# Which rows are gathered when, and on which engine the value products run, in a one-step hybrid decoder

## The chip, the cores and the metric

One core of a Trainium2 chip runs the whole program. Its engines are TensorE (PE; PEld is its weight load), VectorE (DVE), ScalarE (ACT), GpSimd (POOL), which here only issues gathers, and SyncE (SP), which issues all other transfers. The metric is the time of one execution on the device in microseconds, the median of several runs. Everything is single precision. Most matrix products are made of three in a rounded format, each operand being split into a high part (H) and a low rest (L): H by H, H by L, L by H.

## What is computed

A decoder layer over 1024 prompt tokens and 64 sampled tokens: a state-space branch, attention in three dilated windows, a gated mix, an output projection, and then the part that the change touches, a channel mixer that retrieves experts. For each token, eight heads choose 16 of 16384 experts each, so 128 rows of two tables:

```python
eidx = jnp.take_along_axis(cidx, pos, axis=-1).reshape(TOKEN_BLOCK, PEER_HEADS * PEER_TOPK)
gate = jax.nn.softmax(best, axis=-1).reshape(TOKEN_BLOCK, PEER_HEADS * PEER_TOPK)
ue = jnp.take(u_tab, eidx, axis=0)
act = jax.nn.gelu(jnp.einsum('td,tkd->tk', xb, ue))
ve = jnp.take(v_tab, eidx, axis=0)
return jnp.einsum('tk,tkd->td', (gate * act).astype(xb.dtype), ve)
```

The result is added to the layer's input and normalised.

## The kernel before

The tokens go in two halves. The first half is 512 prompt tokens (with the 64 sampled ones up to the attention); the second half is the other 512 and the 64. The second half's experts are computed densely, over all 16384 of them, on TensorE (`dense`); the first half's are gathered, token by token. The gathers are a side stream: the generator `gather` yields after each gathered row, and `tick` advances it by the rate in force (`pace`, the table `RATES`) while the second half's main work is written out. So the order of instructions on each engine is set when the program is built, by these rates and by a scheduler that places the instructions; on the chip each engine then runs its list in order.

The gathered half is four tiles of 128 tokens. For a tile, `gather_u` fetches 128 pieces; a piece is one row of `u_tab` for each of 128 tokens, 512 KB in a buffer `row` (8 buffers, shared by everything gathered), issued by POOL (line 1559). VectorE forms a dot product of each token's row with its input (line 1563, a "dot"). After 128 dots the weights are ready (`act`, line 1569, and for product tiles on TensorE their transpose `wT`).

Then the value rows. There are two ways. In `gather_v` a piece holds one token's 128 rows on 128 partitions (line 1625); for four tokens at a time VectorE copies their weights into `strips` (line 1636) and TensorE forms the products into `va` (line 1641, a "group" of 16 profile entries). In `gather_w`, used for the tiles in `VT`, a piece holds one row for each of 128 tokens (line 1591), and VectorE multiplies it by the token's weight and adds it to the sum `x3v` (line 1597, an "add"). `x3v` is a buffer of the dense loop, so adds can't start before it; there is one such buffer, loaded with the tile's input (line 1587) and sent out after normalising (line 1605). The row of u and the row of v that come next are chosen by a difference of counts, `LEAD`.

The main work beside it, in order: attention of the second half, gated mixing (`glu`), output projection (`w_out`, line 1223), norms, queries (16 chunks: a product, then the top 16 of 128 scores on VectorE, lines 1304 to 1308), the choice of experts (`choose`), the gates (comparisons `oij` on VectorE at line 1392, scaled on ScalarE, multiplied on TensorE, copied into `Gt` and written out; some of the dense scores are computed early between them), and the dense loop (scores, weights `a` times G at line 1442, split at 187, products, accumulation at lines 1464 and 1462), then the last norms (lines 1497 to 1504).

Of the kernel before, what the change touches and what calls it, by code (L numbers as in the profile page):

```python
# [8 lines left out]
I32 = mybir.dt.int32  # L9
# [25 lines left out]
ATICK = 2.8  # L35
LAG, SMB = 4, 5
FILL = (1.1, 2.274, 0.0, 0.8, 1.5, 0.05)
RATES = (1.0, 1.3, 1.0, 1.0, 0.86, 1.0, 0.6)
RB = 8
GL = 20  # L40
GO = (2, 0, 0.7)
LEAD = 160

VT = (2, 3)
SSMT = (10.0, 0.0, 5.0)
NS = 2

# [20 lines left out]
class Prog:  # L68
    def __init__(self, tc, a, stop=None):
        self.tc, self.nc, self.a, self.stop = tc, tc.nc, a, stop  # L70
        self.marks = []
        self.sides, self.inside, self.last, self.dn = {}, False, None, None

    def mark(self, name):
        n = [i.name for i in self.nc.cur_bb.bb.instructions[-1:]]
# [7 lines left out]

        self.sides[name] = [gen, rate, 0.0]

    def pace(self, name, rate):
        if name in self.sides:
            self.sides[name][1] = rate

    def tick(self, us):  # L90
        if self.inside:
# [439 lines left out]
    def mix(self, h):  # L531
        tc, nc = self.tc, self.nc
        nt = NT[h]
        if h == 0:
            self.attn_ahead(0)
        with tc.tile_pool(name=f"at{h}", bufs=1) as ap:
            attn = (ap.tile([128, 4, nt], F32R, name="atH"), ap.tile([128, 4, nt], F32R, name="atL"))
            self.mark(f"attn{h}")
            if h == 0:
                with tc.tile_pool(name="sa", bufs=1) as sp:  # L540
                    self.beside("samples", self.sample_attention(sp), FILL[0])
                    self.attention(h, attn)
                    self.drain("samples")
            else:
                self.pace("gather", RATES[0])
                oa = ap.tile([128, 4, 64], F32, name="oa")
                nc.sync.dma_start(oa, self.oa)
                self.split(attn[0][:, :, 512:], attn[1][:, :, 512:], oa)
                self.attention(h, attn)
                self.pace("gather", RATES[1])  # L550
            with tc.tile_pool(name=f"mx{h}", bufs=1) as mp:
                mix = (mp.tile([128, 8, nt], F32R, name="mixH"), mp.tile([128, 8, nt], F32R, name="mixL"))
                self.mark(f"glu{h}")
                self.glu(h, attn, mix)
                if h == 0:
                    self.es1 = ExitStack()
                    self.ahd1 = [self.es1.enter_context(tc.tile_pool(name=n, bufs=1, side="right")) for n in ("xp1", "pj1")]
                    self.beside("ahead", self.ahead(), FILL[5])
                if h:
                    self.pace("gather", RATES[5])  # L560
                self.mark(f"wout{h}")
                self.espx, px = self.right(f"px{h}")
                self.xf = (px.tile([128, 8, nt], F32R, name="x2H"), px.tile([128, 8, nt], F32R, name="x2L"))
                self.esx2, xp = self.right(f"x2p{h}")
                g = xp.tile([128, D], F32, name="gffn")
                nc.sync.dma_start(g, self.a["g_ffn"].to_broadcast([128, D]))
                x2 = self.w_out(h, mix, xp)
        self.x2sb = xp, g, x2
# [663 lines left out]
    def peer_keys(self, h):  # L1232
        tc, nc, a = self.tc, self.nc, self.a
        v = nc.vector
        nt = NT[h]
        ntl = len(TILES[NT[h]])
        es2 = ExitStack()
        self.pace(*(("gather", RATES[6]) if h else ("ahead", FILL[1])))
        x, (xp, g, x2) = self.xf, self.x2sb
        with ExitStack() as es:  # L1240
            esj = ExitStack()
            jk = esj.enter_context(tc.tile_pool(name=f"jk{h}", bufs=1, side="left" if h else "right"))
            for i in range(ntl):
                rows = 128 if i < 4 else 64
                r0 = h * 512 + i * 128 if i < 4 else 1024
                xn = jk.tile([128, D], F32, name="xn", tag="xn", bufs=2 + h)[128 - rows:]
                self.rms(xp, x2[i][128 - rows:], g[128 - rows:], xn, xn)
                if h == 0:
                    nc.sync.dma_start(self.xn2[r0:r0 + rows], xn)
                self.to_t(xn, rows, x, i * 128, 128 - rows)  # L1250
                self.tick(4.0)
            esj.close()
            self.esx2.close()
            if h:
                da = es.enter_context(tc.tile_pool(name="da", bufs=1))
            with tc.tile_pool(name=f"pk{h}", bufs=1, side="right") as kp, ExitStack() as eg:
                self.pace(*(("gather", RATES[2]) if h else ("ahead", FILL[2])))
                sv = [kp.tile([128, 16, 16], F32, name=f"sv{i}") for i in range(ntl)]
                si = [kp.tile([128, 16, 16], U32, name=f"si{i}") for i in range(ntl)]
                kq = eg.enter_context(tc.tile_pool(name=f"kq{h}", bufs=1, side="right"))  # L1260
                for c in range(16):
                    qp = kq.tile([128, nt], F32, name="qp", tag="qp", bufs=2)
                    keys = kq.tile([128, 128], F32, name="keys", tag="keys", bufs=3)
                    nc.sync.dma_start(keys, a["keys"][:, c])
                    for ps, (c0, c1) in zip(self.gemm_f(a["w_qp"][c], x, SPLITS[NT[h]]), SPLITS[NT[h]]):
                        nc.scalar.copy(qp[:, c0:c1], ps[:, :c1 - c0])
                    pvs = []
                    for i in range(ntl):
                        rows = 128 if i < 4 else 64
                        if i % 4 == 0:  # L1270
                            ps = self.trt()
                        pvs.append(ps[:rows, (i % 4) * 128:(i % 4) * 128 + 128])
                        self.mm(pvs[i], qp[:, i * 128:i * 128 + rows], keys, start=True, stop=True)
                    for i in range(ntl):
                        rows = 128 if i < 4 else 64
                        rest = kq.tile([128, 128], F32, name="rest", tag="rest", bufs=3)[:rows]
                        self.top16(sv[i][:rows, c], si[i][:rows, c], pvs[i], rest)
                    self.tick(6.0)
                    if h and c in CE:
                        self.early(da, x)  # L1280
                self.pace(*(("gather", RATES[3]) if h else ("ahead", FILL[3])))
                eg.close()
                if h:
                    kg = eg.enter_context(tc.tile_pool(name="kg", bufs=1, side="right"))
                for i in range(ntl):
                    rows = 128 if i < 4 else 64
                    self.choose(kp, h, i, rows, sv[i], si[i], (lambda: self.early(da, x)) if h else None)
                    if h == 0:
                        self.tick(30.0)
                    if h == 0 and i == GO[0]:  # L1290
                        self.beside("gather", self.gather(), GO[1])
                    if h:
                        self.gates(kg, i, rows, lambda: self.early(da, x))
            if h:
                self.mark("dense")
                self.pace("gather", RATES[4])
                dn = self.dn = es2.enter_context(tc.tile_pool(name="dn", bufs=1, side="right"))
                self.dense(dn, da, x)
                es2.close()
        self.espx.close()  # L1300
# [206 lines left out]
    def gather(self):  # L1507
# [10 lines left out]
        nu = nv = 0  # L1518
        made = [0, 0]
        while nv < 4:  # L1520
            can = [nu < 4 and nu < nv + 3, nv < nu and (nv not in VT or self.dn is not None)]
            if not any(can):
                yield RATE
                continue
            pick = int(made[0] - made[1] >= LEAD)
            if not can[pick]:
                pick = 1 - pick
            made[pick] += 1
            if next((us[nu] if pick == 0 else ws[nv]), None) is None:
                nu, nv = nu + 1 - pick, nv + pick  # L1530
            else:
                self.catch_up(2)
                yield RATE
# [13 lines left out]
    def gather_u(self, i):  # L1547
# [3 lines left out]
        xn = gp.tile([128, D], F32, name="gxn", tag="gxn", bufs=1)  # L1551
        nc.sync.dma_start(xn, self.xn2[i * 128:(i + 1) * 128])

        ei = self.ei[i] = gp.tile([128, 128], I32, name="ei", tag="ei", bufs=2)
        v.tensor_copy(ei, ef)
        act = gp.tile([128, 128], F32, name="act", tag="act", bufs=3)
        for k in range(128):
# [50 lines left out]
    def gather_v(self, i):  # L1608
# [2 lines left out]

        ps = self.trt()
        nc.tensor.transpose(ps[:, :128], self.peer[0, i][1], self.ident)
        eT = gp.tile([128, 128], I32, name="eT", tag="eT", bufs=2)
        v.tensor_copy(eT, ps[:, :128])
        for hf in range(2):

# [128 lines left out]
```

## Time and profile before

| | us |
|---|---|
| median of 3 runs (3988.77 to 4004.48) | 3997.65 |
| profiled execution | 4006.35 |
| its span | 4004.6 |
| PE busy | 3737.3 |
| DVE busy | 2937.0 |
| POOL busy | 1421.8 |
| dots, x512 (L1563) | 618.0 |
| adds, x256 (L1597) | 327.8 |

Busy time is the time in which an engine has an instruction under way; a mean over the span hides that different stages have different limits. A line of a helper stands for many operations, so the line 80 is most of TensorE's work. The granted clock is 1.00 where TensorE ran at 2.4 GHz throughout.

### The profile page before, as it was taken

Reading aid. Unit: us, or ns where it says so; the run is one execution under the profiler, and the core shown is the slowest. Engines: PE = TensorE matmul, PEld = TensorE weight load, DVE = VectorE, ACT = ScalarE, POOL = GpSimd, SP = SyncE. Lnnn points to the kernel's source line nnn. Section 1 sums busy time; section 2 is a strip of 40 time slices with the busy share of each in tenths; the row PEclk is TensorE's granted clock in tenths of the full one; section 3 lists DMA queues with packets and bytes.
Section 4 is the critical chain, followed back from the end, with each engine's and each line's share of the span. In section 5 each row is a group of like instructions: output and inputs, shape, how many; then the busy total and the mean of one; then the engine's idle time right before and its main releaser. Section 6 shows DMA issues by size and latency. Waiting matters only on the chain.

```text
span 4004.6 us, 72559 instructions
## 1 busy us (share of the span) xinstructions
PE 3737.3 (93%) x27907; PEld 3381.7 (84%) x27907; DVE 2937.0 (73%) x6796; ACT 1430.7 (36%) x2756; POOL 1421.8 (36%) x1236
## 2 busy tenths in 40 slices
PE   8889989899999968799979999989999999999997
PEld 8789965589877755598858899979999999999997
DVE  8626333445994686866889986667767999998998
ACT  3232224323224316322214888842222222222222
POOL 1620000000003434445464354434445665543551
PEclk9999989899999988899989999999999999999999
DMA  5474669544259988799887799999999999998995
GB/s 166 156 227 158 198 234 351 190 139 166 92 189 298 322 321 281 257 350 338 306 313 279 258 344 336 346 347 321 336 335 330 348 343 335 337 335 289 327 331 185
DMA packets 448987, 1112.83 MB, mean 278 GB/s; under 512 B 44656, under 2 KB 189424, under 8 KB 443008
## 3 DMA queue, kind: packets, MB, share of 16 engines
q1 hardware_dynamic: 301184, 571.26, 42.0%
q0 software_dynamic: 147456, 536.94, 37.2%
q8 instruction: 219, 3.59, 0.4%
q14 instruction: 128, 1.05, 0.1%
HBM read 991.77 MB, written 124.27 MB: 279 GB/s over the span
## 4 chain that ended last, share of the span: by engine, by line
PE 74%; DVE 11%; DMA 7%; issue 3%; ACT 3%; POOL 1%; SPq 1%; another core or an unknown queue 0%; ACTq 0%; DVEq 0%; POOLq 0%
PE mm L80 48%; PE tr L80 21%; PE va L1641 2%; DVE row L1563 2%; DMA row<-in_u_tab,ei 1%; DVE wL L136 1%; DMA cc<-in_kc 1%; ACT sm L936 1%; PE tr L954 1%; DMA Q<-Q_scr 1%; PE va L1116 1%; ACT wH L134 1%; DVE st L713 1%; DVE qz L1097 0%; DVE X L714 0%
## 5 line engine op out<-in xcount | busy, mean ns | idle before, releaser
L1559 POOL DMA_INDIRECT row<-in_u_tab,ei x512 | 641.2, 1252 | 966.4 <-DVE row L1563 403.1
L134 ACT CAST wH<-wraw 128x1024 fp32r<-128x1024 f32 (+1 forms) x476 | 492.0, 1035 | 1160.1 <-PE mm L80 823.5
L136 DVE TENSOR_TENSOR wL<-wraw,wH 128x1024 fp32r<-128x1024 f32 (+1 forms) x476 | 578.3, 1215 | 385.9 <-ACT wH L134 367.0
L1563 DVE SCALAR_TENSOR_TENSOR row<-row,gxn 128x1024 f32<-128x1024 f32 x512 | 618.0, 1219 | 42.7 <-DMA row<-in_u_tab,ei 34.7
L80 PE MATMUL tr<-x2H,wH 128*128 128x288 f32 x2048 | 614.8, 301 | 7.2 <-ACT a L1408 5.4
L80 PE MATMUL tr<-x2L,wH 128*128 128x288 f32 x2048 | 611.8, 299 | 0.0
L80 PE MATMUL tr<-x2H,wL 128*128 128x288 f32 x2048 | 608.1, 299 | 0.0
L80 PE MATMUL mm<-WH,wH 128*128 128x288 f32 (+2 forms) x2048 | 495.7, 295 | 2.5 <-ACT WH L186 1.9
L80 PE MATMUL mm<-WL,wH 128*128 128x288 f32 (+2 forms) x2048 | 496.1, 295 | 1.0 <-DVE WL L187 1.0
L80 PE MATMUL mm<-WH,wL 128*128 128x288 f32 (+2 forms) x2048 | 489.6, 294 | 0.0
L1591 POOL DMA_INDIRECT row<-in_v_tab,ei x256 | 350.3, 1368 | 361.6 <-DVE x3v L1597 301.6
L1625 POOL DMA_INDIRECT row<-in_v_tab,eT x256 | 316.8, 1238 | 366.8 <-DVE row L1563 198.5
L80 PEld LDWEIGHTS tr<-x2H,wH 128*128 128x128 f32 x2048 | 386.8, 189 | 17.4 <-ACT a L1408 8.0
L80 PEld LDWEIGHTS tr<-x2L,wH 128*128 128x128 f32 x2048 | 386.8, 189 | 3.4 <-issue 3.4
L80 PEld LDWEIGHTS tr<-x2H,wL 128*128 128x128 f32 x2048 | 385.8, 189 | 2.7 <-issue 2.5
L80 PEld LDWEIGHTS mm<-WH,wH 128*128 128x128 f32 x2048 | 347.7, 188 | 10.8 <-issue 4.1
L80 PEld LDWEIGHTS mm<-WL,wH 128*128 128x128 f32 x2048 | 349.3, 188 | 4.6 <-issue 3.4
L80 PEld LDWEIGHTS mm<-WH,wL 128*128 128x128 f32 x2048 | 346.6, 188 | 1.7 <-issue 1.7
L1597 DVE SCALAR_TENSOR_TENSOR x3v<-row,act,x3v 128x1024 f32<-128x1024 f32 x256 | 327.8, 1280 | 1.0
L80 PE MATMUL mm<-xnH,wH 128*128 128x288 f32 (+1 forms) x960 | 323.1, 337 | 0.0
L80 PE MATMUL mm<-xnH,wL 128*128 128x288 f32 (+1 forms) x960 | 320.5, 334 | 2.7 <-DVE wL L136 2.7
L80 PE MATMUL mm<-xnL,wH 128*128 128x288 f32 (+1 forms) x960 | 320.0, 333 | 0.0
(392 smaller groups left out, 7781.3 us busy)
## 6 DMA issues: line engine op xcount, KB each, us to landing
wraw<-in_vT SPq DMA_DIRECT2D x132, 512.0 KB
wraw<-in_uT SPq DMA_DIRECT2D x128, 512.0 KB
G_scr<-Gt SPq DMA_DIRECT2D x18, 2048.0 KB
G<-G_scr SPq DMA_DIRECT2D x32, 1152.0 KB
cc<-in_kc SPq DMA_DIRECT2D x48, 512.0 KB
cc<-in_vc SPq DMA_DIRECT2D x48, 512.0 KB
wraw<-in_w_g SPq DMA_DIRECT2D x32, 512.0 KB
wraw<-in_w_qp SPq DMA_DIRECT2D x32, 512.0 KB
```

Of the source, the lines that this page charges most:

```text
L80: self.last = self.nc.tensor.matmul(out, lhsT=lhsT, rhs=rhs, **kw)
L134: nc.scalar.copy(h, raw)
L136: nc.vector.tensor_sub(l, raw, h.bitcast(F32))
L713: v.tensor_mul(t2[hi], w(p[lo]), w(a[1][lo]))
L936: nc.scalar.activation(sm[:, hd, 256 - nk:], sm[:, hd, 256 - nk:], AF.Exp, scale=0.125, bias=stat[:, i, 2, c], accum_out=stat[:, i, 1, c])
L954: nc.tensor.transpose(ps[:, (h2 * 2 + j) * 128:(h2 * 2 + j + 1) * 128], sm[:, 2 * hp + h2, c:c + 128], self.ident)
L1559: self.after(nc.gpsimd.indirect_dma_start(out=row, out_offset=None, in_=a["u_tab"], in_offset=bass.IndirectOffsetOnAxis(ap=ei[:, k:k + 1], ...
L1563: self.after(v.scalar_tensor_tensor(row, row, 1.0, xn, op0=ALU.mult, op1=ALU.mult, accum_out=act[:, k:k + 1]))
L1591: self.after(nc.gpsimd.indirect_dma_start(out=row, out_offset=None, in_=a["v_tab"], in_offset=bass.IndirectOffsetOnAxis(ap=ei[:, k:k + 1], ...
L1597: self.after(v.scalar_tensor_tensor(x3, row, self.gw[i][:, k:k + 1], x3, op0=ALU.mult, op1=ALU.add))
L1625: self.after(nc.gpsimd.indirect_dma_start(out=row, out_offset=None, in_=a["v_tab"], in_offset=bass.IndirectOffsetOnAxis(ap=eT[:, tk:tk + 1 ...
L1641: self.after(nc.tensor.matmul(va[0][c:c + 32, :], lhsT=self.strips[:, s, j, 31 - t - s:63 - t - s], rhs=rows[s * 2 + j][:, b * 512:(b + 1) ...
```

## The change

Tile 1 moves from `gather_v` to `gather_w`: of the four tiles, three now have their value products on VectorE and only tile 0 on TensorE. Each rate now carries a wish, "u", "v" or none. With a wish the next row is of that kind if it can be; value rows of a tile are held back until its dots are `LATE` rows old. The wish is "u" in the second half's attention, and "v" from the output projection to the end of the queries. Without a wish the old rule holds. A third buffer holds the row numbers of a tile (`ei`), the transposed ones need only one (`eT`).

```diff
-RATES = (1.0, 1.3, 1.0, 1.0, 0.86, 1.0, 0.6)
+RATES = ((1.0, "u"), (1.2, None), (1.0, "v"), (0.9, None), (0.9, None), (1.0, "v"), (0.7, "v"))
...
 LEAD = 160
-
-VT = (2, 3)
+LATE = 12
+
+VT = (1, 2, 3)
...
-    def pace(self, name, rate):
+    def pace(self, name, rate, want=None):
         if name in self.sides:
             self.sides[name][1] = rate
+            if name == "gather":
+                self.want = want
...
-        self.pace(*(("gather", RATES[6]) if h else ("ahead", FILL[1])))
+        self.pace(*(("gather", *RATES[6]) if h else ("ahead", FILL[1])))
...
-            pick = int(made[0] - made[1] >= LEAD)
+            if nu < 4 and self.want == "v":
+
+                can[1] = can[1] and (not can[0] or made[0] >= 128 * nv + 128 + LATE)
+            pick = int(made[0] - made[1] >= LEAD) if self.want is None else int(self.want == "v")
             if not can[pick]:
                 pick = 1 - pick
...
-        ei = self.ei[i] = gp.tile([128, 128], I32, name="ei", tag="ei", bufs=2)
+        ei = self.ei[i] = gp.tile([128, 128], I32, name="ei", tag="ei", bufs=3)
...
-        eT = gp.tile([128, 128], I32, name="eT", tag="eT", bufs=2)
+        eT = gp.tile([128, 128], I32, name="eT", tag="eT", bufs=1)
```

Behind the diff the numbers of the lines are three to six higher: dots are line 1569, adds 1603, top-16 steps 1307 to 1311, the late norms 1505 and 203.

POOL before, in the gates: u rows and v rows of tile 1 in turn (`ei`: one row number for each of 128 tokens; `eT`: the 128 rows of one token).

```order
L1559 DMA row_17597<-in_u_tab,ei_15584 128x1024
L1625 DMA row_17599<-in_v_tab,eT_16395 128x1024
L1559 DMA row_17601<-in_u_tab,ei_15584 128x1024
L1625 DMA row_17647<-in_v_tab,eT_16395 128x1024
L1559 DMA row_17649<-in_u_tab,ei_15584 128x1024
L1625 DMA row_17717<-in_v_tab,eT_16395 128x1024
```

POOL after, from the output projection to the dense loop, where x97 and the like count rows that follow one another:

```order
L1565 DMA row<-in_u_tab,ei 128x1024
L1631 DMA row<-in_v_tab,eT 128x1024 x97
L1565 DMA row<-in_u_tab,ei 128x1024 x197
L1597 DMA row<-in_v_tab,ei 128x1024 x102
L1565 DMA row<-in_u_tab,ei 128x1024
L1597 DMA row<-in_v_tab,ei 128x1024
```

The turn-taking is gone there: the v rows of tile 0 stand in one block, then 197 u rows, then 102 v rows of tile 1, by VectorE's layout.

VectorE before, in the last chunks of the queries (MAX and MAX_INDEX are the top-16 steps):

```order
L1308 MAX_INDEX si_18748<-sv_18743,rest 128x8
L1563 SCALAR_TENSOR_TENSOR row,act<-row,gxn 128x1024
L1307 MAX sv_18744<-rest 128x8
L1307 MAX sv_18745<-rest 64x8
L1308 MAX_INDEX si_18749<-sv_18744,rest 128x8
L1308 MAX_INDEX si_18750<-sv_18745,rest 64x8
L1563 SCALAR_TENSOR_TENSOR row,act<-row,gxn 128x1024 x2
L1636 COPY strips<-wT 128x4
L1563 SCALAR_TENSOR_TENSOR row,act<-row,gxn 128x1024
L1304 MAX sv_18741<-tr 128x8
```

VectorE after, at the same place:

```order
L1569 SCALAR_TENSOR_TENSOR row,act<-row,gxn 128x1024 x4
L1307 MAX sv_18738<-tr 128x8
L139 TENSOR_TENSOR wL<-wraw,wH 128x1024
L1307 MAX sv_18742<-tr 64x8
L1569 SCALAR_TENSOR_TENSOR row,act<-row,gxn 128x1024
L1308 MAX_INDEX si_18743<-sv_18738,tr 128x8
L1309 MATCH_REPLACE rest<-sv_18738,tr 128x128
L1307 MAX sv_18739<-tr 128x8
L1569 SCALAR_TENSOR_TENSOR row,act<-row,gxn 128x1024
L1308 MAX_INDEX si_18747<-sv_18742,tr 64x8
L1569 SCALAR_TENSOR_TENSOR row,act<-row,gxn 128x1024
```

The strip copies are over, and the dots stand closer, up to four in a row, between the same steps; in the earlier chunks there are none.

VectorE before, from the last accumulation on (`acc`; G is a tile of the late norms):

```order
L1462 TENSOR_TENSOR acc<-acc,mm 128x256 x2
L214 SCALAR_TENSOR_TENSOR ss<-ss 64x1
L215 SCALAR_TENSOR_TENSOR ss<-ss 64x1
L200 SCALAR_TENSOR_TENSOR G<-G,ss 64x1024
L1502 TENSOR_TENSOR G<-G,mm 128x512 x4
L206 TENSOR_SCALAR ss<-ss 128x1
L207 TENSOR_SCALAR ss<-ss 128x1
```

VectorE after, some way behind its last accumulation:

```order
L1603 SCALAR_TENSOR_TENSOR x3v<-row,act,x3v 128x1024
L218 SCALAR_TENSOR_TENSOR ss<-ss 128x1 x2
L217 SCALAR_TENSOR_TENSOR ss<-ss 64x1
L1603 SCALAR_TENSOR_TENSOR x3v<-row,act,x3v 128x1024
L203 SCALAR_TENSOR_TENSOR G<-G,ss 128x1024 x2
L218 SCALAR_TENSOR_TENSOR ss<-ss 64x1
L1603 SCALAR_TENSOR_TENSOR x3v<-row,act,x3v 128x1024
L203 SCALAR_TENSOR_TENSOR G<-G,ss 64x1024
L1603 SCALAR_TENSOR_TENSOR x3v<-row,act,x3v 128x1024 x6
L1505 TENSOR_TENSOR G<-G,mm 128x512 x2
L1603 SCALAR_TENSOR_TENSOR x3v<-row,act,x3v 128x1024
```

Adds of tile 3 now stand among the late norms, 22 of them behind the last accumulation.

## Rows read from the trace of the kernel before

**Rows 1.** The page: busy time of each engine, and the gathers' queue.

```profile
PE 3737.3 (93%) x27907; PEld 3381.7 (84%) x27907; DVE 2937.0 (73%) x6796; ACT 1430.7 (36%) x2756; POOL 1421.8 (36%) x1236
...
q0 software_dynamic: 147456, 536.94, 37.2%
```

**Rows 2.** Stage, us; busy PE, PEld, DVE, ACT, POOL; clock, DMA share, GB/s.

```profile
1703.80:1830.60 126.80, 126.80 (x965) 115.59 (x964) 83.47 (x140) 29.49 (x44) 59.80 (x56) 1.00 0.92 337
1830.60:1900.20 69.60, 64.95 (x527) 58.21 (x525) 40.89 (x105) 13.03 (x17) 34.91 (x32) 0.98 0.95 353
1900.20:1929.60 29.40, 23.91 (x153) 20.39 (x154) 23.12 (x66) 9.40 (x18) 14.13 (x13) 0.83 0.89 326
1929.60:2120.70 191.10, 160.72 (x1101) 131.36 (x1102) 174.96 (x802) 30.48 (x53) 113.36 (x93) 0.89 0.89 308
2120.70:2169.30 48.60, 46.81 (x355) 41.67 (x354) 47.99 (x222) 18.30 (x27) 27.79 (x20) 1.00 0.94 333
2169.30:2300.00 130.70, 126.62 (x986) 119.86 (x985) 122.87 (x340) 104.65 (x226) 40.90 (x27) 0.99 0.71 237
2300.00:2641.80 341.80, 338.69 (x2680) 314.85 (x2680) 254.62 (x374) 291.12 (x644) 159.54 (x116) 1.00 0.97 341
2641.80:2696.40 54.60, 43.77 (x302) 39.05 (x302) 27.53 (x43) 15.79 (x26) 18.80 (x18) 0.87 0.98 377
2696.40:3983.60 1287.20, 1286.67 (x9734) 1257.45 (x9733) 1118.07 (x1681) 342.14 (x476) 623.00 (x487) 1.00 0.89 322
3983.60:4004.60 21.00, 0.71 (x7) 0.48 (x5) 9.95 (x39) 2.30 (x4) 0.00 (x0) 0.61 0.40 140
```

**Rows 3.** Waits (us, times, longest): TensorE 1900-2700, 2690-3990; VectorE 2160-2700.

```profile
PE tr L80 <- DVE rest L1306: 22.3, 6, 7.5
PE va L1641 <- DMA row<-in_v_tab,eT: 13.6, 5, 7.9
...
PE mm L80 <- DVE G L1502: 0.5, 1, 0.5
...
DVE oij L1392 <- PE mm L80: 52.3, 51, 3.3
```

**Rows 4.** Tile va: shortest, median and longest in ns, first and last start.

```profile
L1641 PE MATMUL va<-row,strips x1024: 589/592/1063, 1712.7 to 3053.1; 128*32 128x512 f32 x171
```

**Rows 5.** Chain of waits, 2630 to 2700 (start, us, engine, what, line).

```profile
2631.61 1.85 PE va L1641 x16
...
2653.50 1.92 PE va L1641 x16
...
2659.75 17.32 DMA row<-in_u_tab,ei
```

**Rows 6.** VectorE by time (start, us), and the strip copies.

```profile
2647.92 1.22 DVE L1563 SCALAR_TENSOR_TENSOR row<-row,gxn 128x1024 f32<-128x1024 f32 x1
...
2649.06 1.22 DVE L1563 SCALAR_TENSOR_TENSOR row<-row,gxn 128x1024 f32<-128x1024 f32 x1
...
3602.53 1.28 DVE L1597 SCALAR_TENSOR_TENSOR x3v<-row,act,x3v 128x1024 f32<-128x1024 f32 x1
...
3633.28 3.92 DVE L1597 SCALAR_TENSOR_TENSOR x3v<-row,act,x3v 128x1024 f32<-128x1024 f32 x3
...
3924.88 1.27 DVE L1597 SCALAR_TENSOR_TENSOR x3v<-row,act,x3v 128x1024 f32<-128x1024 f32 x1
3926.07 1.42 DVE L187 TENSOR_TENSOR WL<-a,WH 128x576 fp32r<-128x576 f32 x2
...
L1636 DVE COPY strips<-wT x64: 140/171/401, 1703.8 to 3034.5; 128x4 f32<-128x4 f32 x64
```

**Rows 7.** Busy time in the middle of the dense loop, and in its last eighth.

```profile
3100.00:3500.00 400.00, 400.00 (x3023) 400.00 (x3022) 375.34 (x541) 104.52 (x148) 234.67 (x169) 1.00 0.93 342
3822.70:3983.60 160.90, 160.37 (x1218) 160.13 (x1217) 150.24 (x244) 45.47 (x62) 56.30 (x46) 1.00 0.75 265
```

**Rows 8.** The chain of waits by time, behind the last accumulation.

```profile
3993.93 1.06 ACT acc L198
```

More of the change, by code (lines that the diff above doesn't have):

```diff
@@ L71, in __init__ @@
         self.marks = []
-        self.sides, self.inside, self.last, self.dn = {}, False, None, None
+        self.sides, self.inside, self.last, self.dn, self.want = {}, False, None, None, None
     def mark(self, name):
@@ L544, in mix @@
             else:
-                self.pace("gather", RATES[0])
+                self.pace("gather", *RATES[0])
                 oa = ap.tile([128, 4, 64], F32, name="oa")
@@ L549, in mix @@
                 self.attention(h, attn)
-                self.pace("gather", RATES[1])
+                self.pace("gather", *RATES[1])
             with tc.tile_pool(name=f"mx{h}", bufs=1) as mp:
@@ L559, in mix @@
                 if h:
-                    self.pace("gather", RATES[5])
+                    self.pace("gather", *RATES[5])
                 self.mark(f"wout{h}")
@@ L1256, in peer_keys @@
             with tc.tile_pool(name=f"pk{h}", bufs=1, side="right") as kp, ExitStack() as eg:
-                self.pace(*(("gather", RATES[2]) if h else ("ahead", FILL[2])))
+                self.pace(*(("gather", *RATES[2]) if h else ("ahead", FILL[2])))
                 sv = [kp.tile([128, 16, 16], F32, name=f"sv{i}") for i in range(ntl)]
@@ L1280, in peer_keys @@
                         self.early(da, x)
-                self.pace(*(("gather", RATES[3]) if h else ("ahead", FILL[3])))
+                self.pace(*(("gather", *RATES[3]) if h else ("ahead", FILL[3])))
                 eg.close()
@@ L1295, in peer_keys @@
                 self.mark("dense")
-                self.pace("gather", RATES[4])
+                self.pace("gather", *RATES[4])
                 dn = self.dn = es2.enter_context(tc.tile_pool(name="dn", bufs=1, side="right"))
```

## The prediction

> **What bounds the kernel now.** I read the page's table of engines first [rows 1]: TensorE is busy 93% of the span, VectorE 73%, so one average hides stages with different limits. Then I cut the second half at instructions that stand in both versions (the first strip copy, the end of the gated mixing, of the output projection and of the norms, the first and last gate comparison, the first and last accumulation of the dense loop) and asked for busy time in each stretch [rows 2]. The reader is to see four regimes. The dense loop, 1287.2 us, has TensorE at 1286.67 and weight loads at 1257: TensorE bounds it. The queries, 191.1 us, have VectorE at 174.96 (92%), TensorE at 160.72, and a granted clock of 0.89, so TensorE stops and starts. The gates have TensorE at 97% and 99%; their first part has VectorE at 94%, their second the DMA engines at 0.97. The last 21 us belong to VectorE and a few loads. The table of TensorE's waits [rows 3] names the queries' limit, top-16 searches on VectorE (22.3 us); in the dense loop TensorE waits 0.5 us in all.
>
> **The change, part by part.** All counts below are of VectorE's order in the two versions between the same instructions.
>
> TensorE loses half of the va products: 1024 entries in the profile [rows 4] are 64 groups of 16, and a group takes 1.85 to 1.92 us on the chain of waits [rows 5], so 32 groups are 60 us. Groups before and after: mixing 8 and 7, output projection 4 and 7, norms to choice 15 and 18, gates and the step into the dense loop 20 and 0, dense loop 17 and 0. So 37 us leave the gates and 32 us the dense loop, and 9 us are added between projection and choice.
>
> VectorE gains 128 adds and loses 32 strip copies (0.17 us each, [rows 6]). A dot starts 1.14 us after the one before it, an add 1.19 us before what follows it, or 1.32 us where the next add needs its result (three in 3.92 us, of which the last has its full 1.28) [rows 6]. The dots move too. Dots before and after: mixing 30 and 30, output projection 15 and 2, norms 7 and 0, queries and choice 55 and 50, gates with the step 80 and 147, dense 167 and 125. Adds: 10 already in the step, 352 in the dense loop against 256, and 22 behind its last accumulation, where before had none. POOL's gathers stay 1024 of 512 KB each (536.94 MB in the gathers' queue [rows 1]), and by stage they differ little (queries and choice 111 and 110, gates with the step 160 and 157, dense 491 and 477), so the DMA load is nearly the same; only its last 22 rows come late.
>
> Mixing: TensorE is busy throughout, one group fewer, -2. Output projection: its 64.95 us of TensorE become 71 in a stretch of 69.6; I take +3 (bounds +1 and +8). Norms: -1.
>
> Queries and choice: on average 5 dots fewer, some 6 us, but the order is uneven. For about 12 of the 16 query chunks no dot runs, and 15 groups of four rows do; then 33 dots stand in the last four. A chunk takes 191.1/16 = 11.9 us now. The first 12 have, on TensorE, (160.72 - 11 x 1.85)/16 = 8.8 us a chunk and 15 groups, 134 us at the low clock of this stretch; on VectorE 12 x (174.96 - 46 x 1.14)/16 = 92; on the DMA engines 60 rows and 12 weight tiles of 512 KB, 107 us at the 353 GB/s of [rows 2]. I take 122 for 143: -21. The last four have 4 x 7.7 + 33 x 1.14 = 68 us on VectorE, 70 to 74 with its usual gaps, for 48: I take +21. Together nothing (bounds -16, if VectorE's total alone counts, and +12, if TensorE waits for the v rows as it did five times for 13.6 us [rows 3]). Choice: 17 dots for 9 with VectorE at 99%, some of it given back by three groups fewer on TensorE: +4.
>
> Gates and the step into the dense loop, together 527.1 us: TensorE falls from 509 to 472. VectorE rises from 405 by 67 x 1.14 = 76 and 10 x 1.2 = 12, less the copies, to 490. So the busiest engine changes. At the share that VectorE sustained beside a full TensorE, 94% (375.34 of 400, [rows 7]), 490 us need 521; at the 97% that TensorE had here, 507. The DMA engines, at 0.97 in the second part, get 3 rows fewer. I take -10 (bounds -27, with VectorE at 98%, and +15, with waits that leave it at 90%). The 17.32 us for which one dot waits on its row in the step, with TensorE's weights behind it [rows 5], can stay or go; it lies within these bounds.
>
> Here the row says that TensorE is the busiest before, VectorE after. The Trainium skill (Perfetto Trace Analysis, Identifying the Most-Contended Engine) says that occupancy is a fair measure of the limit for the Vector engine, that matmul busy time isn't one for TensorE, and that weight-load time should be used there. The row agrees in direction: weight loads are 474 of these 527 us, below the matmuls' 509. By the rule the 37 us taken from TensorE there would be worth 6 to 20 us, as in the sum; by matmul time they would all come back.
>
> Dense loop: TensorE loses 32 us and is the bound. The cover is VectorE: 1118 - 42 x 1.14 + 96 x 1.22 less small things is some 1180 of 1255, 94%, which is what [rows 7] shows beside a full TensorE for 400 us. The last eighth is tighter: 51 adds for 42 on 150.24 of 160.9, 98%; I charge 2 us. The one buffer x3v now turns over twice in the loop (sum out, next tile in, adds stopped); before, adds stopped from 3603.8 to 3633.3 us with TensorE full, so it costs nothing unless SP's queue holds the load. Sum -30 (bounds -34 and -5).
>
> Tail: behind the last accumulation the order has 22 adds among the norms of the last tiles. With 8 row buffers, the first 8 rows are there, the rest follow as adds free buffers: 22 x 1.5 us (add with the small norm steps between, or 512 KB at 353 GB/s) is 33 us. Then that tile's square, norm steps, scaling and output, as from 3993.93 to the end [rows 8], some 11 us. 44 against 21: +23 (bounds +15 and +35). SP's queue also puts the load of the scale into a row buffer, which waits for an add, ahead of the last x_scr load; that load then lands about when the adds end, within the same 33 us.
>
> Sum: -2 + 3 - 1 + 0 + 4 - 10 - 30 + 23 = -13. The profiled execution took 4006.35 us, 8.7 above the median of the runs; it becomes 3993, and against the median of 3997.65 the forecast is 3985.
>
> **Rivals.** First, the stages come near their floors: queries -16, gates -27 (500 us, VectorE at 98%), dense -32, tail +18, output projection +1, mixing and norms -3, choice 0: -59, 3939. For it: VectorE held 99% through the choice [rows 2]. Against it: comparisons, scaling and products pass from engine to engine in the gates, and VectorE waits 52.3 us on products within them [rows 3]. Chance 0.22.
>
> Second, VectorE becomes the bound, in the gates and the dense loop. Its price: a stage needs its VectorE time over 0.92, the share of the queries. Gates 490/0.92 = 533, +6; dense 1180/0.92 = 1283, -4; queries +12, choice +8, tail +30 as rows queue up: +52, 4050; it turns slower than before once VectorE can't keep 93.5%, where gates and dense loop together give only the 27 us that the tail and the rest take (1670 of 1787 us). For it: the burst of dots in the queries, dots that wait in order for rows with everything behind them. Against: 94% held for 400 us [rows 7]. Chance 0.17, at a middle of 4030.
>
> Third, the change does what it says and nothing comes of it: gates and dense loop give 30 instead of 40, the queries cost 2, the tail 23 and the rest 4: 3997. For it, the tail is the surest cost of all; against it, so is TensorE's loss in the dense loop. Chance 0.18. My own forecast with its neighbourhood, 3970 to 3993, has 0.43.
>
> **How the numbers follow.** A difference under 0.5%, 20 us, is what a measurement of this kernel can't tell from none. My forecast lies inside it, 7 us from its edge, so a third of its 0.43 falls beyond. Faster: 0.22 from the first rival and 0.15 from mine, 0.37. Same: 0.28 from mine and the third rival's 0.18, 0.46. Slower: the second, 0.17. The range leaves out the far half of the first rival and of the second: 3938 to 4025. The likeliest case's own is 3965 to 4000.
>
> **What would show it.** Dense loop from first to last accumulation: 1257 if right, 1280 or more with idle TensorE behind VectorE if the second rival is. Gates with the step: 517, with VectorE over 93%; 490 speaks for the first rival. Queries: no dots and TensorE waiting on v rows first, then four chunks of over 15 us. Tail: 22 adds and 44 us from the last accumulation to the end. Wrong would be a TensorE that waits over 10 us in the dense loop, or a tail under 30 us.

## The result, and the profile after

The changed kernel takes 4045.81 us (median of 4 runs, 4041.33 to 4048.84) against 3994.5 for the one before in the same comparison: a ratio of 1.0117, 95% interval 1.0099 to 1.0134. By that ratio it is slower by some 47 us (the two medians lie 51 apart), and it is above the range of the forecast, whose upper end was 4025. The profiled execution has a span of 4046.0, 41.4 more than before.

The page's line of engines, to be held against [rows 1], is the first warning: TensorE works 50 us less, VectorE 137 more.

```profile
PE 3686.8 (91%) x27393; PEld 3380.6 (84%) x27393; DVE 3073.6 (76%) x6870; ACT 1432.1 (35%) x2752; POOL 1508.5 (37%) x1236
```

Busy time by stage, the stages cut at the same instructions as in [rows 2] (the two parts of the gates in one; columns as there):

```profile
1707.50:1833.20 125.70, 125.70 (x958) 114.50 (x957) 81.06 (x138) 29.25 (x43) 62.06 (x56) 1.00 0.93 337
1833.20:1901.20 68.00, 67.90 (x567) 57.75 (x569) 28.07 (x80) 12.81 (x16) 26.58 (x28) 1.00 0.92 338
1901.20:1930.50 29.30, 24.83 (x177) 18.85 (x170) 17.03 (x58) 9.74 (x19) 9.96 (x9) 0.94 0.74 269
1930.50:2128.60 198.10, 157.82 (x1150) 127.36 (x1150) 164.65 (x795) 31.69 (x53) 123.87 (x100) 0.89 0.91 316
2128.60:2181.80 53.20, 45.44 (x330) 45.24 (x330) 52.10 (x200) 15.83 (x25) 26.02 (x18) 0.92 0.86 305
2181.80:2694.60 512.80, 473.22 (x3551) 462.51 (x3550) 454.01 (x852) 404.18 (x879) 243.58 (x138) 0.96 0.83 285
2694.60:2744.50 49.90, 19.32 (x113) 18.39 (x112) 34.20 (x46) 10.14 (x19) 28.96 (x19) 0.60 0.96 350
2744.50:3995.90 1251.40, 1249.01 (x9438) 1248.21 (x9437) 1163.50 (x1605) 340.79 (x469) 640.42 (x478) 1.00 0.91 326
3995.90:4046.00 50.10, 0.94 (x9) 0.70 (x7) 42.80 (x112) 3.44 (x6) 19.70 (x15) 0.55 0.70 254
```

Subtract the stages of [rows 2]: output projection and mixing -2.7, norms -0.1, queries +7.0, choice +4.6, gates +40.3, step -4.7, dense loop -35.8, tail +29.1; the first of them begins 3.7 later. Together 41.4. So the dense loop gave what it was to give, and the gates and the tail took it, with more. In the gates neither engine is full: TensorE at 92%, VectorE at 89%, where before TensorE had 98%. ScalarE, which scales the comparisons, stands between the two: TensorE waits for it 38.4 us in the gates (7.7 before), and it waits for VectorE's comparisons 23.2 us (7.0 before).

The queries in four equal parts:

```profile
1930.50:1980.00 49.50, 47.64 (x360) 36.78 (x360) 39.33 (x228) 9.47 (x16) 26.98 (x26) 1.00 0.93 330
1980.00:2030.00 50.00, 50.00 (x381) 37.75 (x379) 36.59 (x211) 8.72 (x15) 24.39 (x27) 1.00 0.93 339
2030.00:2080.00 50.00, 43.80 (x330) 37.51 (x326) 41.79 (x173) 11.73 (x19) 31.67 (x25) 0.96 0.92 308
2080.00:2128.60 48.60, 16.38 (x85) 15.32 (x86) 46.94 (x186) 1.77 (x3) 40.83 (x25) 0.61 0.84 287
```

No dot runs in the first half, and VectorE has room (39 of 49.5 us). The 33 dots begin at 2053.5: 12 stand in the third part and 21 in the last, where VectorE is at 97% and TensorE is busy for 16 of 49 us, at a granted clock of 0.61. TensorE's waits from queries to choice name it (us, times, longest; 22.3 in [rows 3]):

```profile
PE tr L81 <- DVE rest L1309: 38.0, 3, 15.3
```

In gates and step, VectorE waits for products less than before (52.3, [rows 3]) and for loads more (5.7 before):

```profile
DVE oij L1395 <- PE mm L81: 33.5, 25, 3.2
DVE row L1569 <- DMA gxn<-xn_scr: 16.4, 2, 15.1
DVE row L1569 <- DMA row<-in_u_tab,ei: 12.9, 5, 6.8
```

Where in the gates? I cut them at every 18th of the 144 comparisons. Seven of the eight pieces (the first with the choice ahead of it) differ from before by -7 to +9 us; the one from the 36th to the 54th takes 89.0 us for 64.4:

```profile
2309.70:2398.70 89.00, 80.85 (x613) 78.94 (x612) 80.81 (x185) 57.62 (x122) 55.21 (x28) 1.00 0.90 309
```

VectorE's groups in it (busy us, mean ns; then idle time before them) begin with 28 dots, the first 28 of tile 2, where before had 12:

```profile
L1569 DVE SCALAR_TENSOR_TENSOR row<-row,gxn 128x1024 f32<-128x1024 f32 x28 | 33.5, 1217 | 6.3 <-DMA row<-in_u_tab,ei 5.0 <-DMA gxn<-xn_scr 1.3
L1395 DVE TENSOR_TENSOR oij<-i,T 128x1024 f32<-128x1024 f32 x18 | 21.6, 1215 | 1.8 <-PE mm L81 1.8
```

The same stretch holds the choice of experts for the last 64 tokens, eight searches and the positions, which is VectorE's work too; before, that choice stood there as well.

The tail's chain of waits (start, us): a norm step, then an add that the next one stands behind (x3v, 1.27 us in VectorE's order; the chain gives 1.05 us of it as "issue"), and again; then the output and the last load.

```profile
4002.58 0.21 DVE ss L218 x2
4002.80 0.07 DVE ss L217
4002.87 0.07 DVE x3v L1603
4002.94 1.05 issue
4003.99 0.21 DVE ss L216 x2
...
4017.37 6.30 DMA out_ys<-G
4023.72 6.72 DMA G<-x_scr
```

Output and load take 6.30 and 6.72 us beside the last gathers; before they took 3.00 and 4.28. That is the 6 us by which the tail is longer than forecast.

### The profile page after: what moved, and what is told of

The parts are those of the page before. It is cut to its first block, busy times and chain, and to the rows that moved or that the text cites. A ratio compares the mean times of both kernels' runs of the same rounds, so it can differ in the third digit from the quotient of the medians.

```text
span 4046.0 us, 71541 instructions
## 1 busy us (share of the span) xinstructions
PE 3686.8 (91%) x27393; PEld 3380.6 (84%) x27393; DVE 3073.6 (76%) x6870; ACT 1432.1 (35%) x2752; POOL 1508.5 (37%) x1236
## 4 chain that ended last, share of the span: by engine, by line
PE 65%; DVE 13%; DMA 8%; issue 6%; ACT 3%; POOL 3%; SPq 1%; POOLq 0%; DVEq 0%; ACTq 0%
PE mm L81 44%; PE tr L81 17%; DVE row L1569 3%; DVE wL L139 1%; DMA row<-in_u_tab,ei 1%; POOL row L1565 1%; PE va L1647 1%; DVE x3v L1603 1%; DMA cc<-in_kc 1%; ACT wH L137 1%; DMA M_scr<-kst 1%; PE tr L957 1%; ACT Gt L1400 1%; PE va L1119 1%; ACT sm L939 1%
## 5 line engine op out<-in xcount | busy, mean ns | idle before, releaser
L1565 POOL DMA_INDIRECT row<-in_u_tab,ei x512 | 744.4, 1454 | 1037.7 <-DVE row L1569 573.4
L1597 POOL DMA_INDIRECT row<-in_v_tab,ei x384 | 517.9, 1349 | 505.4 <-DVE x3v L1603 379.2
L1603 DVE SCALAR_TENSOR_TENSOR x3v<-row,act,x3v 128x1024 f32<-128x1024 f32 x384 | 491.5, 1280 | 3.3 <-DMA x3v<-x_scr 1.6
```

The source lines that it names most:

```text
L1565: self.after(nc.gpsimd.indirect_dma_start(out=row, out_offset=None, in_=a["u_tab"], in_offset=bass.IndirectOffsetOnAxis(ap=ei[:, k:k + 1], ...
L1597: self.after(nc.gpsimd.indirect_dma_start(out=row, out_offset=None, in_=a["v_tab"], in_offset=bass.IndirectOffsetOnAxis(ap=ei[:, k:k + 1], ...
L1603: self.after(v.scalar_tensor_tensor(x3, row, self.gw[i][:, k:k + 1], x3, op0=ALU.mult, op1=ALU.add))
```

## The experiments

Nine kernels beside the two, most with one line changed. The table gives the stages in us, cut as above, from each one's profiled execution, and the ratio of the times to the kernel before, with its 95% interval; "gates" also has dots and strip groups by VectorE's order, "36-54" the stretch from the start of the 36th comparison to that of the 54th, "adds" the adds behind the last accumulation.

| kernel | queries | choice | gates (dots/groups) | 36-54 | step | dense | tail (adds) | ratio, interval |
|---|---|---|---|---|---|---|---|---|
| before | 191.1 | 48.6 | 472.5 (70/18) | 64.4 | 54.6 | 1287.2 | 21.0 (0) | 1 |
| changed | 198.1 | 53.2 | 512.8 (138/0) | 89.0 | 49.9 | 1251.4 | 50.1 (22) | 1.0117 (1.0099-1.0134) |
| old_rates | 189.1 | 48.7 | 482.2 (119/5) | 69.0 | 57.0 | 1252.6 | 40.8 (12) | 0.9996 (0.9983-1.0008) |
| two_tiles | 198.1 | 52.9 | 485.4 (90/11) | 85.6 | 58.6 | 1295.3 | 21.7 (0) | 1.0113 (1.0092-1.0133) |
| no_wish | 190.1 | 53.9 | 490.1 (117/6) | 65.8 | 49.1 | 1254.7 | 49.7 (22) | 1.0019 (1.0009-1.0028) |
| wish_q | 181.0 | 65.0 | 522.1 (137/0) | 95.6 | 50.4 | 1251.0 | 49.4 (22) | 1.0127 (1.0102-1.0151) |
| slow_gates | 199.3 | 51.3 | 505.8 (119/0) | 82.7 | 49.7 | 1258.1 | 72.4 (38) | 1.0125 (1.0108-1.0142) |
| gxn_pool | 200.7 | 53.9 | 508.5 (137/0) | 90.6 | 50.8 | 1256.2 | 50.4 (22) | 1.0130 (1.0111-1.0148) |
| short_dots | 198.3 | 45.9 | 434.6 (123/0) | 56.5 | 55.2 | 1252.2 | 65.2 (34) | 0.9948 (0.9933-0.9963) |
| short_lump | 199.6 | 52.6 | 479.7 (139/0) | 59.3 | 48.1 | 1255.4 | 49.7 (22) | 1.0039 (1.0026-1.0052) |
| early_rows | 183.6 | 54.1 | 502.2 (134/4) | 75.8 | 55.1 | 1249.2 | 23.7 (0) | 1.0010 (0.9997-1.0023) |

The part ahead of the mixing, in which several of these have the same order, ends between 1694 and 1709 us, so totals of single profiles are not compared to better than that; stages and ratios are.

**The two halves of the change apart.** Theory A was that moving the tile overloads VectorE in the gates, theory B that the wishes do it, theory C that transfers are late there.

old_rates:

```diff
-RATES = ((1.0, "u"), (1.2, None), (1.0, "v"), (0.9, None), (0.9, None), (1.0, "v"), (0.7, "v"))
+RATES = ((1.0, None), (1.3, None), (1.0, None), (1.0, None), (0.86, None), (1.0, None), (0.6, None))
```

> Three tiles on VectorE as in the changed kernel, but the six old rates and no wish: the two halves of the change apart. VectorE's order has 144 dots and 5 strip groups from the first comparison to the first accumulation (147 and 0 in the changed kernel, 80 and 20 in the one before), 55 dots in queries and choice as before, 12 adds behind the last accumulation for 22. Theory A, VectorE's load (the moved tile's value rows can't be added before the dense loop, so the gates' rows turn into dots, and VectorE sets the gates): 545 to 565 us from first comparison to first accumulation, queries and choice back to 240, tail 38, in all 4015 to 4030. Theory B, the wishes' order (dots pushed out of the queries and packed in runs are what holds the gates up): 535 us or less there, in all 3995 or less. Theory C, waits for transfers (a tile's input, single rows), gives no number here but its waits would have to stand in the trace again.

Measured: no difference from before. Gates, step, dense loop, tail:

```profile
2165.50:2647.70 482.20, 465.50 (x3628) 452.69 (x3627) 434.35 (x812) 405.96 (x879) 243.68 (x143) 1.00 0.91 315
2647.70:2704.70 57.00, 20.06 (x128) 19.13 (x128) 39.99 (x66) 11.79 (x22) 29.66 (x22) 0.64 0.90 331
2704.70:3957.30 1252.60, 1248.18 (x9426) 1247.03 (x9427) 1166.34 (x1583) 339.43 (x468) 616.69 (x479) 1.00 0.90 325
3957.30:3998.10 40.80, 0.91 (x9) 0.68 (x7) 32.19 (x101) 3.45 (x6) 5.52 (x5) 0.58 0.54 182
```

Gates with step take 539.2 us, 12 more than before, the tail 20 more, the dense loop 35 less: the move of the tile alone comes out even. By number the stage lay between A and B; by total (a median of 3998.58) it was near B's 3995. A falls as the main cause.

two_tiles:

```diff
-VT = (1, 2, 3)
+VT = (2, 3)
```

> The new rates and wishes, but only tiles 2 and 3 on VectorE as before. 100 dots and 14 strip groups between first comparison and first accumulation, no add behind the last accumulation, dense loop with 18 groups on TensorE. A: 525 to 542 us for the gates with the step, dense 1287, tail 21, queries and choice 11 longer than before; 4000 to 4018 in all. B: the gates with the step stay at 555 to 565 and the total is 4030 or more.

Gates, dense loop, tail:

```profile
2175.70:2661.10 485.40, 463.56 (x3574) 442.70 (x3573) 399.14 (x765) 402.20 (x872) 204.18 (x130) 0.97 0.84 291
2719.70:4015.00 1295.30, 1289.73 (x9752) 1257.94 (x9751) 1120.15 (x1692) 342.63 (x476) 635.62 (x496) 1.00 0.89 324
4015.00:4036.70 21.70, 1.10 (x6) 0.70 (x4) 11.04 (x38) 2.30 (x4) 0.00 (x0) 0.50 0.47 160
```

The loss is there without the moved tile, as B has it, but in other places than B gave: gates with step 544, which is 17 us more than before, with 21 more in the stretch from the 36th to the 54th comparison alone (28 dots); queries and choice 11 more, the dense loop 8. The last of these I can't explain. So the moved tile changes nothing under the old order (0.9996) and nothing under the new one either (1.0117 for 1.0113).

**Which part of the rates.** no_wish:

```diff
-RATES = ((1.0, "u"), (1.2, None), (1.0, "v"), (0.9, None), (0.9, None), (1.0, "v"), (0.7, "v"))
+RATES = ((1.0, "u"), (1.2, None), (1.0, None), (0.9, None), (0.9, None), (1.0, None), (0.7, None))
```

> The changed kernel with its new rates, the wish "v" taken out (output projection, norms, queries); the wish "u" of the attention stays. By VectorE's order: 45 dots and 11 strip groups in the queries (33 and 15 in the changed kernel), 117 dots and 6 groups in the gates (138 and 0), 8 dots in the step, still 22 adds behind the last accumulation. Theory H1, the number of dots (the wish brings v rows forward and pushes dots back into the gates, where VectorE is at 88% or more, and each costs 1.1 to 1.5 us; the queries lose time as their dots come in one lump): queries with choice 240 (251.3 in the changed kernel), gates with step 530 to 542 (562.7), tail still 48 to 51; in all 4003 to 4015. Theory H2, the rates (0.9 for 1.0 in the gates, 1.2 for 1.3 in the mixing, 0.9 for 0.86 in the dense loop) are what costs: gates with step stay over 550 and the total over 4030.

As expected of the wish: queries with choice 244, gates with step 539.2, ratio 1.0019. So the wish "v" costs 1.0117 - 1.0019, some 39 us (give or take 8, by the intervals); the other rates (with the wish "u") 1.0019 - 0.9996, some 9 (give or take 6), with the tail's ten further adds; the moved tile nothing. That these parts add up to the whole proves nothing, since each is a difference to the next kernel; what bears them out is two_tiles.

wish_q:

```diff
-RATES = ((1.0, "u"), (1.2, None), (1.0, "v"), (0.9, None), (0.9, None), (1.0, "v"), (0.7, "v"))
+RATES = ((1.0, "u"), (1.2, None), (1.0, "v"), (0.9, None), (0.9, None), (1.0, None), (0.7, None))
```

> The changed kernel with the wish "v" in the queries alone (none in the output projection and the norms, whose dots return: 13 and 7 for 2 and 0). By the order the queries then hold 10 dots and 19 strip groups (33 and 15; 45 and 11 without the wish, which took 190), choice 22 dots (17), gates 137 (138), tail 22. If VectorE's work sets the queries: 23 dots fewer are 26 us, so 170 to 180 us there, choice 57 to 60; gates and step 555 to 565; in all 4025 to 4035. If the wait of the searches and products for one another does, and TensorE with its groups: 188 to 198, in all 4042 to 4055.

Queries and choice:

```profile
1926.50:2107.50 181.00, 169.54 (x1266) 133.27 (x1266) 139.19 (x743) 34.02 (x57) 92.82 (x86) 0.97 0.91 317
2107.50:2172.50 65.00, 37.72 (x276) 37.17 (x275) 60.55 (x222) 12.68 (x21) 37.41 (x27) 0.81 0.85 314
```

By the queries it lies between the two, by its total (4048.7) it is the second: the queries fall to 181 with VectorE at 77% and TensorE, with 19 groups, at 94%; the choice takes 65 and the gates 522. What leaves the queries is paid behind them, and the wish in the queries alone costs as much (1.0127) as in all its stages.

**Work, or waits for transfers.** short_dots forms the dots between choice and dense loop over 64 columns:

```diff
...
+                self.short = 64 if h else D
                 self.pace(*(("gather", *RATES[3]) if h else ("ahead", FILL[3])))
...
+                self.short = D
                 self.pace("gather", *RATES[4])
...
-                self.after(v.scalar_tensor_tensor(row, row, 1.0, xn, op0=ALU.mult, op1=ALU.mult,
+                n = self.short
+                self.after(v.scalar_tensor_tensor(row[:, :n], row[:, :n], 1.0, xn[:, :n], op0=ALU.mult, op1=ALU.mult,
...
```

> The changed kernel, with each dot between the choice and the dense loop formed over 64 of its 1024 columns (the other columns are left out of those products); rows, waits and order of the gathers are kept. This takes some 144 x 1.05 = 150 us of VectorE's 488 there. A: 500 to 520 us from first comparison to first accumulation, TensorE at 95% or more in the gates. C (the waits for rows and for the tile's input set the gates, not the work): 545 to 560. The tail has 34 adds by the order, so the end comes 14 us later than it would.

Gates and step:

```profile
2173.80:2608.40 434.60, 432.51 (x3415) 429.80 (x3415) 307.70 (x776) 400.19 (x869) 153.68 (x123) 1.00 0.92 319
2608.40:2663.60 55.20, 35.58 (x248) 34.76 (x246) 19.35 (x63) 15.59 (x26) 20.77 (x22) 0.81 0.99 382
```

489.8 us for 562.7, shorter than the 500 to 520 of A; TensorE is at 99.5% of the gates. So VectorE's work holds them up. It is not a clean parting of work from arrival: 15 dots fewer stand in these gates (123 for 138), and the 12.9 us for which VectorE stood for rows are gone with the work.

gxn_pool:

```diff
-        nc.sync.dma_start(xn, self.xn2[i * 128:(i + 1) * 128])
+        nc.gpsimd.dma_start(xn, self.xn2[i * 128:(i + 1) * 128])
```

> The changed kernel, with a tile's input for the dots (gxn) loaded through POOL's queue instead of SyncE's, where it landed 15.7 us after the last dot of the tile before it and VectorE stood for 15.14 us. C: gates with the step 547 or less, in all 4030. A: most of those 15 us come back too, since VectorE was idle in them, if the load takes 4 us or less; if it only moves the wait (POOL's gathers stand behind it), 556 to 563 and 4040 to 4046.

Nothing gained; VectorE still stands for that load once:

```profile
DVE row L1569 <- DMA gxn<-xn_scr: 13.3, 1, 13.3
```

Against 15.1 through SyncE: changing the queue doesn't cure it. Through SyncE the issue alone took 11.47 us, with the DMA engines busy throughout (share 1.03 from 2701.5 to 2713.0); through POOL it stood behind four row gathers, was issued 4.7 us after the last dot and landed 9.3 us later. What would shorten it stays open. The loss isn't there in any case, since the step with this wait in it is shorter than before (49.9 us for 54.6).

**How many dots, or where.** slow_gates:

```diff
-RATES = ((1.0, "u"), (1.2, None), (1.0, "v"), (0.9, None), (0.9, None), (1.0, "v"), (0.7, "v"))
+RATES = ((1.0, "u"), (1.2, None), (1.0, "v"), (0.77, None), (0.9, None), (1.0, "v"), (0.7, "v"))
```

> The changed kernel with the gates' rate at 0.77 for 0.9, all wishes kept: 119 dots in the gates (138), as many as with the old rates, none of them beside value products on TensorE; 38 adds behind the last accumulation (22). H1: gates 478 to 492 us (512.8 in the changed kernel, 482.2 with the old rates), queries with choice still 251, tail 68 to 72 by 1.3 us for an add; in all 4030 to 4045. If it is not the number but that rows of one kind follow one another there: gates 505 or more, in all 4060.

The number alone fails: with as many dots as old_rates (119) the gates take 505.8 for 482.2, although VectorE has 3 us less to do than there.

```profile
2178.60:2684.40 505.80, 463.98 (x3543) 456.01 (x3542) 431.41 (x799) 405.19 (x876) 219.41 (x119) 0.99 0.80 271
```

Of these 24 us, 14 lie between the 36th and 54th comparison. Elsewhere the engines wait for one another (VectorE for products, 32.1 in old_rates' gates):

```profile
DVE oij L1395 <- PE mm L81: 54.3, 33, 4.1
```

What brings these waits on stays open. So the number of dots isn't all. By its figures (505.8 us, 4057 in all) this is what was expected if rows of one kind in a row are what costs; old_rates has five strip groups among its dots, slow_gates none, and the run can't tell that from the crowded place. short_lump takes the work out of that one place and leaves its rows, all of one kind, as they are:

```diff
-                self.after(v.scalar_tensor_tensor(row, row, 1.0, xn, op0=ALU.mult, op1=ALU.mult,
+                n = 64 if i == 2 and k < 28 else D
+                self.after(v.scalar_tensor_tensor(row[:, :n], row[:, :n], 1.0, xn[:, :n], op0=ALU.mult, op1=ALU.mult,
...
```

> The changed kernel; only the first 28 dots of the third tile are formed over 64 of 1024 columns (the rest left out). They are the 28 that stand between the 36th and the 54th comparison, where VectorE also has the last choice of experts (8 searches and the positions), and where the changed kernel takes 89.1 us and the old rates, with 17 dots there, 67.8. If the lump of VectorE's work in that stretch is the cause: 62 to 70 us there, gates 485 to 495 (512.8), in all 4018 to 4028. If it is the rows' arrival (two waits of 2.5 us, gathers of one kind in a row), the stretch keeps 80 us or more, and the total stays over 4035. If the gates give it back later, because VectorE or the rows are behind anyway: stretch shorter, gates 505 or more.

The stretch, then all gates:

```profile
2299.10:2359.50 60.40, 60.03 (x474) 59.68 (x473) 55.38 (x184) 52.90 (x118) 37.59 (x25) 1.00 1.02 368
2171.60:2651.30 479.70, 459.24 (x3552) 453.53 (x3550) 427.79 (x854) 405.35 (x879) 220.75 (x138) 0.99 0.87 305
```

The stretch (here with one comparison more than in the table) falls from 89.0 us to 60.4, and the gates fall by 33.1, more than was expected: nothing is given back later, and rows of one kind don't hold this stretch up. VectorE has 26.2 us less to do in the gates; the other 7 are idle time of VectorE, which no longer stands 12.9 us for rows but some 6 us more for TensorE and ScalarE. The same stretch in old_rates (one comparison less), where 17 dots stand in it:

```profile
2291.30:2359.20 67.90, 65.93 (x521) 60.77 (x519) 64.75 (x153) 53.91 (x113) 46.29 (x25) 1.00 0.99 329
```

Over all kernels with whole dots the stretch takes 64 to 69 us with 12 to 17 dots in it, and 76 to 96 with 20 to 28. That the same 28 dots would have cost less elsewhere in the gates is argued from this and from slow_gates against old_rates; no run shortened 28 dots at another place.

**A version that might beat both.** early_rows:

```diff
-RATES = ((1.0, "u"), (1.2, None), (1.0, "v"), (0.9, None), (0.9, None), (1.0, "v"), (0.7, "v"))
+RATES = ((1.15, None), (1.3, None), (1.0, None), (1.0, None), (0.86, None), (1.0, None), (0.6, None))
```

> Three tiles on VectorE, no wish, and the old rates but 1.15 for 1.0 in the attention: by the order five dots more before the output projection, 134 and 16 dots in gates and step (119 and 25 with the old rates), no add behind the last accumulation (12). H1: tail 21 for 41, gates with step 545 to 552 for 539; in all 3982 to 3992, which would be faster than both kernels. Against it: if the six more dots cost 2 us or more each and the dense loop, with VectorE over 93%, takes 5 to 10 us longer, 3998 or more.

Gates and tail:

```profile
2176.40:2678.60 502.20, 475.00 (x3606) 459.38 (x3604) 452.12 (x850) 405.33 (x882) 277.26 (x151) 0.98 0.89 311
3982.90:4006.60 23.70, 1.27 (x12) 1.03 (x10) 12.98 (x47) 2.30 (x4) 0.00 (x0) 0.60 0.41 147
```

The tail is gone as expected, 17 us. But gates with step take 557.3 us, above the 545 to 552 expected (the gates 20 more than in old_rates for 15 dots more, 1.33 us each), and mixing to norms 11 more. No gain: what left the tail was paid for ahead of it. Of the versions that compute the whole result, none beat the kernel before.

## Why the prediction was wrong

**Gates with the step** is the step that failed: "At the share that VectorE sustained beside a full TensorE, 94% (375.34 of 400, [rows 7]), 490 us need 521", and from it "I take -10 (bounds -27, with VectorE at 98%, and +15, with waits that leave it at 90%)". VectorE's work was right: 454.01 + 34.20 = 488.2 us. The share wasn't: 488.2 of 562.7 is 86.8%, and the stage grew by 35.6. Of the 74.5 us for which VectorE stood, 33.5 were for products, 29.3 for loads and 10.1 for ScalarE; 94% would have left 31 in all. The 94% came from the dense loop, where, as I read it, the work of VectorE is spread evenly and little hangs on it close behind. In the gates it comes in lumps: of the 147 dots, 28 stand where VectorE also has the last choice. I had that order before me, counted it by stage, and looked for crowding only in the queries. Short_lump shows 33 of the 40 us of the gates to hang on 28 dots; short_dots, with gates and step shorter than before the change (489.8 us for 527.1), that VectorE's work bounds the rest too.

**Queries and choice**: the course was as told in part, no dots first and then 33. By the first search of each chunk, the first twelve chunks took 126.8 us (139.0 before), where I took 122 for 143; the last four took 71.3 (52.1 before), within my 70 to 74. But TensorE did not wait on v rows first (1.9 us in all): it was busy for 97.6 of the first 99.5 us. The size lay between its bounds: +7.0 where I took 0, and +4.6 for 4 in the choice.

**Dense loop**: -35.8 for -30, TensorE at 99.8%. The cover held: VectorE at 93%, as forecast at 94.

**Tail**: +29.1 for +23; the load and the output beside the gathers make the difference. Over these kernels it grows by 1.3 to 1.7 us for an add.

**Sum**: -13 forecast, +41.4 in the profile; of the 54 missed, 45.6 lie in the gates with the step, 7 in the queries, 6 in the tail and 4 ahead of the mixing; dense loop and output projection gave 10 more than forecast.

The second rival's 4050 came near by total, and its mechanism came true in the gates, where VectorE became the bound, but at a lower share than its 92%: it gave gates with step +6, measured +35.6, and the dense loop almost no gain (-4, measured -36). So its closeness is luck in part: the two misses cancel.

The signs that I named for being wrong didn't come (TensorE waits 2.5 us in the dense loop, and the tail takes 50.1): both watched stages whose account held. The sign that spoke was the gates', 517 us with VectorE over 93%.

Of the Trainium skill's rule (Perfetto Trace Analysis, Identifying the Most-Contended Engine), the part on matmul time agrees: with 37 us of products gone, TensorE's busy time in gates and step fell by 16.5 (509 to 492.5), and to 468 once VectorE was relieved in short_dots; busy time there wasn't a sum of work. Weight-load time, which it would use instead, was no sum of work here either: it rose from 473.8 us to 480.9, with some 300 loads fewer. And the 6 to 20 us that I drew from the rule did not come.

## What to carry to other kernels

Count a moved instruction by place, not by stage: hold the order of the in-order engine beside what else it has in that very stretch, and price it with the share that this stage shows, not with that of a calmer one. Where a change has a move and a new order in it, run each alone before explaining the sum: here the move was free and the order cost it all. And where an engine has little room in every stage that follows, look where work that leaves one stage goes: in wish_q dots left the queries and in early_rows adds left the tail, and both were paid for in other stages.

## What the hardware showed

POOL's issue of a gather slows where VectorE is full, though the gather's rows and size are the same. POOL in order of time, in the crowded stretch (start, us):

```profile
2335.76 1.02 POOL L1565 DMA_INDIRECT row<-in_u_tab,ei  x1 [0.31 <-issue]
2338.93 11.19 POOL L1565 DMA_INDIRECT row<-in_u_tab,ei  x1 [2.14 <-DVE look L1333]
...
2354.63 0.93 POOL L1565 DMA_INDIRECT row<-in_u_tab,ei  x1 [0.30 <-issue]
```

One issue took 11.19 us (the longest in these gates took 13.98), where the shortest take 0.93, at a time when VectorE had no gap (10.00 of 10 us in each of three windows, 2320 to 2350); a little later two dots waited for their rows, 5.0 us together. The mean over the gates is 1771 ns in the changed kernel,

```profile
L1565 POOL DMA_INDIRECT row<-in_u_tab,ei x138 | 244.4, 1771 | 275.7 <-DVE row L1569 234.9 <-issue 25.0 <-DVE pos L1308 8.2
```

and 1256 ns with the short dots, where VectorE is at 71%:

```profile
L1568 POOL DMA_INDIRECT row<-in_u_tab,ei x123 | 154.5, 1256 | 281.8 <-DVE row L1573 251.6 <-issue 13.7 <-DVE best L1313 9.7
```

Issue by issue in the changed gates, the 98 during which VectorE was busy for over 95% took 1.88 us on average, the 22 with VectorE busy for under half 0.94. It isn't the kind of row: behind the gates, two v rows issued beside dots (2698.01 and 2700.30) took 1.99 us each, the next three, with VectorE idle, 0.94, 0.94 and 0.93. So a full VectorE also delays the rows that it will want next. VectorE stood 12.9 us for rows in the changed gates, and not at all in those of short_lump and short_dots; how much of the gates' loss comes by this way was not taken apart.
